# One encoder layer on one Trainium2 core: the first stage in blocks of 256 weight columns with fixed orders, and the forget gates' running sum on the Vector engine

## The chip, the cores and the metric

The kernel is one program on one core of a Trainium2 chip. A core has five engines that run side by side and meet only at semaphores: TensorE (PE; matmuls and transposes; its weight loads are listed as PEld), VectorE (DVE), ScalarE (ACT), GpSimd (POOL) and SyncE (SP, here used to issue DMAs). Data moves from HBM to the on-chip memory SBUF by DMA; TensorE writes only to PSUM, which has eight banks of 512 float32 columns on 128 partitions, and ACT and DVE read it from there. Each engine works through its own instruction stream in order: an instruction that waits holds up everything behind it on its engine.

The metric is the device time of one execution in microseconds (us). The time before is the median of three runs.

## The reference

The reference is one layer of a streaming encoder on 512 tokens of width 1024, in float32. Cut to what matters here:

```
h = rms_norm(x, norm_mix_pre)
a_q, a_k, a_v, f_q, f_k, f_v, f_g, c_u, s_x, s_b, s_c = split(h @ w_in)      # 5640 columns
ya = diff_attention(...);  ya = rms_norm(ya) * (1 - lambda_init)              # branch A, 4 heads
log_f = log_sigmoid(f_g + b_fgt);  c = cumsum(log_f, tokens)                  # branch F, 8 heads
yf = softmax(q k^T * scale + c[q] - c[k], causal) v
c_a, c_g = split(c_u + b_glu)                                                 # branch C
yc = silu(layer_norm(causal_depthwise_conv31(c_a * sigmoid(c_g))))
ys = s_b * causal_depthwise_conv3(s_c * s_x)                                  # branch S
mixed = sum_n sigmoid(h @ w_gate + b_gate)[n] * (branch[n] @ w_branch[n]) @ w_out
x = x + rms_norm(mixed);  cross-attention into 256 memory tokens;  gated MLP with a 3-tap conv
```

The change touches the first norm, the first products for `c_a` and `c_g`, and the running sum `c` of the eight forget gates over the tokens.

## The kernel before, in words

**Precision.** Every float32 operand of a product is split in two: `hi`, the value rounded to the matmul's fast format (a cast on ACT), and `lo`, what is left of it (a subtraction on DVE, sometimes on POOL). One product then is three passes on TensorE, hi x hi, hi x lo and lo x hi, accumulated in one PSUM bank (`mm3`, through `matmul`, L175). Weights come in pieces of 512 KB: `load_raw` (L120) issues the DMA on SP into one of two buffers `wr`; `split_weights` makes `wh` (L135, ACT) and `wl` (L136, on DVE or POOL), four buffers each.

**Layout.** Activations lie with channels on the partitions, as `ht` = (`hth`, `htl`), eight groups of 128 channels by 512 tokens. A token tile of x (128 tokens x 1024) is normed (`normed`: square sum on ACT L210, `rstd_of` on POOL L201 and L204, multiplication by the norm and by the gain on DVE L214), transposed by TensorE in groups of four 128x128 blocks (`to_channels`, `transpose` L179), and split from PSUM (`split`: ACT L109, DVE L110).

**Stages.** `all_jobs` lists the jobs of the layer; `run_blocks` loads and splits the weights of a job two jobs ahead and then runs its body. Work that isn't tied to weights (the convolution's 31 taps on DVE, attention heads, norms) is cut into pieces in a `Background` queue, which gives out pieces by a clock that counts the columns of the matmuls issued.

**What sets the order.** A planner arranges each engine's instructions by a simulated timeline, unless the kernel keeps some of them in the order of the program. In the kernel before, only ACT's instructions for the first two token tiles and the first weight cast are kept that way (`pin`), together with the DMAs of the small parameter rows (L298).

**First stage.** SP loads the gain row (L245), x tiles 0 and 1 (L247), the first 128 columns of the weights for `c_a`, and x tiles 2 and 3. TensorE spreads the gain row over the partitions (L256). Tiles 0 and 1 are normed and transposed. Then the first three blocks of `c_jobs` (128 columns of `c_a`, 128 of `c_g`, the next 128 of `c_a`) are multiplied with the first 256 tokens alone; tiles 2 and 3 are normed and transposed between them. After the third block the parameter rows are loaded (`load_rows`, L298) and transposed (`finish_init`), and the three blocks get the second 256 tokens. From the fourth block on a block takes all 512 tokens at once. `done` (L363, L366, L367) evacuates a block, and each finished pair of blocks starts a convolution task (L411, L415).

**Forget gates.** `forget_gates` computes the log-sigmoid on [128 tokens x 4 tiles x 8 heads] and then the sum over the tokens: four float32 products with a triangle of ones `tri` (L691) give [8 heads x 512 tokens] in PSUM. ACT scales it (L692), POOL writes it to DRAM as `crows` (L693), from where each pair of heads gets it spread over the partitions (`ck`, L710); four small transposes (L696) and a copy (L697) make `cq`. `f_task` builds the bias from both (POOL, L740 and L742) and adds it to the scores (DVE, L746).

## Time and profile before

| | us |
|---|---|
| median of three runs | 1111.14 |
| the three runs | 1110.30, 1112.38, 1111.14 |
| the profiled execution, its time | 1112.67 |
| the profiled execution, its span | 1111.0 |
| TensorE busy in that span | 1093.0 |
| DVE, ACT, POOL busy in that span | 690.5, 465.4, 107.4 |

The span is the time from the first to the last instruction that the profiler shows; the execution's own time has 1.67 us around it. In the profile, a group is named by line, engine and operation, then `out<-in` by the program's names and shapes. Matmuls are pipelined, so that the distance between two starts, and not the length of one, is the rate. The chain of waits is followed back from the last instruction, at each step to what released it. Idle time of an engine that is not the bottleneck costs nothing.

### The profile page before, as it was taken

The page shows a single profiled execution, that of the slowest core. Times are in us where ns is not written, and L with a number is a line of the kernel's source. Part 1 is how long each engine was busy: PE and PEld are TensorE (multiplying, and loading weights), DVE is VectorE, ACT ScalarE, POOL GpSimd, SP SyncE. Part 2 cuts the span into 40 slices and gives each one's busy share as a digit, 9 for nine tenths or more (in the row PEclk, how much of TensorE's full clock was granted, in tenths as well). Part 3 has the DMA queues.
Part 4 walks back from the last instruction along what each step waited for, and adds up shares of the span by engine and source line. Part 5 has one row for each costly group of instructions (what it writes and reads, how often), then busy time and mean ns, then how long its engine had stood idle before and what let it go on. Part 6 is the DMA issues. An engine that isn't in the chain of part 4 may idle for free.

```text
span 1111.0 us, 14146 instructions
## 1 busy us (share of the span) xinstructions
PE 1093.0 (98%) x5419; PEld 913.2 (82%) x5419; DVE 690.5 (62%) x1123; ACT 465.4 (42%) x783; POOL 107.4 (10%) x199
## 2 busy tenths in 40 slices
PE   7999999999999999999999999999999999999997
PEld 6888888887878978888888889888888888888886
DVE  4899985457665357767464477677666666642224
ACT  5322222467564255545442355454444444431112
POOL 3000001000101025323010130120000000000001
PEclk9999999999999999999999999999999999999999
DMA  6433433331212233333262252233333333332322
GB/s 176 119 93 97 104 89 94 95 95 58 76 58 77 77 115 95 96 95 92 79 201 89 90 171 97 94 95 113 96 95 95 95 95 95 95 95 95 95 76 76
DMA packets 147896, 109.29 MB, mean 98 GB/s; under 512 B 3647, under 2 KB 135340, under 8 KB 147829
## 3 DMA queue, kind: packets, MB, share of 16 engines
q1 hardware_dynamic: 145269, 99.85, 30.6%
q0 software_dynamic: 2560, 8.54, 2.7%
q8 instruction: 43, 0.70, 0.3%
q14 instruction: 24, 0.20, 0.1%
HBM read 106.27 MB, written 2.11 MB: 98 GB/s over the span
## 4 chain that ended last, share of the span: by engine, by line
PE 94%; DVE 2%; DMA 1%; POOL 1%; issue 1%; ACT 1%; POOLq 0%; DVEq 0%; SPq 0%; ACTq 0%
PE ps_mm L175 81%; PE ps_sc L175 7%; PE ps_tr L179 3%; PE ps_tr L175 3%; DVE wl L136 1%; POOL st_r L204 1%; DVE res L912 1%; DMA wr<-in_w_xkv 0%; DMA wr<-in_w_xq 0%; DMA xs<-in_x 0%; ACT nt L210 0%; POOL wl L136 0%; PE ps_sc L691 0%; ACT wh L135 0%; DVE e L579 0%
## 5 line engine op out<-in xcount | busy, mean ns | idle before, releaser
L175 PE MATMUL ps_mm<-hth,wh 128*128 128x512 f32 (+1 forms) x984 | 373.5, 380 | 1.6 <-ACT wh L135 1.2
L175 PE MATMUL ps_mm<-hth,wl 128*128 128x512 f32 (+1 forms) x984 | 373.0, 379 | 0.8 <-POOL wl L136 0.8
L175 PE MATMUL ps_mm<-htl,wh 128*128 128x512 f32 (+1 forms) x984 | 372.8, 379 | 0.3 <-DVE htl L110 0.3
L136 DVE TENSOR_TENSOR wl<-wr,wh 128x1024 fp32r<-128x1024 f32 (+1 forms) x180 | 221.4, 1231 | 231.4 <-ACT wh L135 228.5
L135 ACT CAST wh<-wr 128x1024 fp32r<-128x1024 f32 (+1 forms) x182 | 190.9, 1049 | 369.8 <-PE ps_mm L175 215.5
L175 PEld LDWEIGHTS ps_mm<-hth,wl 128*128 128x128 f32 x984 | 185.9, 189 | 36.3 <-POOL wl L136 1.0
L175 PEld LDWEIGHTS ps_mm<-hth,wh 128*128 128x128 f32 x984 | 185.9, 189 | 36.2 <-ACT wh L135 1.4
L175 PEld LDWEIGHTS ps_mm<-htl,wh 128*128 128x128 f32 x984 | 186.3, 189 | 34.8 <-DVE htl L110 0.5
L415 DVE SCALAR_TENSOR_TENSOR y<-y,par,y 128x482 f32<-128x482 f32 (+25 forms) x120 | 82.5, 729 | 0.2
L175 PE MATMUL ps_mm<-y,wh 128*128 128x512 f32 x256 | 80.9, 395 | 0.0
L352 DVE SCALAR_TENSOR_TENSOR c<-ps_mm,par,c 128x510 f32<-128x510 f32 x84 | 62.6, 746 | 1.4
L175 PEld LDWEIGHTS ps_mm<-y,wh 128*128 128x128 f32 x256 | 47.5, 188 | 9.9
L175 PE MATMUL ps_mm<-y,wl 128*128 128x512 f32 x128 | 50.8, 397 | 0.0
L201 POOL TENSOR_SCALAR st_m<-pm 128x1 f32<-128x1 f32 x12 | 2.6, 219 | 459.6 <-ACT junk L1164 349.2
L109 ACT CAST acth<-c 128x512 fp32r<-128x512 f32 x22 | 13.7, 620 | 54.8 <-DVE c L1111 54.8
L740 POOL TENSOR_SCALAR fbias<-ck,cq 128x128 f32<-128x128 f32 (+3 forms) x32 | 28.9, 907 | 69.9 <-DVE st L746 62.3
L175 PE MATMUL ps_mm<-wh,actl 128*128 128x512 f32 x88 | 34.6, 393 | 0.0
L175 PE MATMUL ps_mm<-wl,acth 128*128 128x512 f32 x88 | 34.6, 393 | 0.0
L175 PE MATMUL ps_mm<-wh,acth 128*128 128x512 f32 x88 | 34.2, 392 | 0.0
L109 ACT CAST pth<-ps_tr 128x512 fp32r<-128x512 f32 (+3 forms) x56 | 23.5, 450 | 23.9 <-PE ps_tr L179 22.6
L1105 ACT ACTIVATE c<-ps_mm,par 128x512 f32<-128x512 f32 x42 | 32.5, 773 | 0.0
L175 PE MATMUL ps_sc<-qk 128*128 128x128 f32 (+3 forms) x128 | 29.9, 329 | 1.1 <-DVE st L579 0.9
(268 smaller groups left out, 1573.5 us busy)
## 6 DMA issues: line engine op xcount, KB each, us to landing
wr<-in_w_up SPq DMA_DIRECT2D x44, 512.0 KB
wr<-in_w_in SPq DMA_DIRECT2D x40, 512.0 KB
wr<-in_w_gate SPq DMA_DIRECT2D x32, 512.0 KB
wr<-in_w_down SPq DMA_DIRECT2D x22, 512.0 KB
wr<-in_w_branch SPq DMA_DIRECT2D x16, 512.0 KB
wr<-in_w_out SPq DMA_DIRECT2D x8, 512.0 KB
wr<-in_w_xkv SPq DMA_DIRECT2D x8, 512.0 KB
wr<-in_w_in SPq DMA_DIRECT2D x4, 520.0 KB
```

The lines of the kernel that those rows point to most:

```text
L109: order(A.copy(hi, ps))
L135: order(A.copy(hi[:, :n], raw[:, :n]))
L136: low.tensor_tensor(lo[:, :n], raw[:, :n], hi[:, :n].bitcast(F32), ALU.subtract)
L175: PE.matmul(ps, lhs, rhs, start=start, stop=stop)
L179: PE.transpose(ps, x, ident[:n, :n])
L201: G.tensor_scalar(m, parts[0], EPS, None, ALU.add)
L204: G.tensor_tensor(r, m, nhalf[:, :n], ALU.pow)
L352: V.scalar_tensor_tensor(dst[:, s:], src[:, :S - s], w(k), dst[:, s:], ALU.mult, ALU.add)
L415: V.scalar_tensor_tensor(dst[:, s:], src[:, :S - s], pc("conv_dw", k * 4 + j), dst[:, s:], ALU.mult, ALU.add)
L740: G.tensor_scalar(bias[:, :w], ck[j][:, :w], -1.0, cq[:, qt, head:head + 1], ALU.mult, ALU.add)
L912: V.scalar_tensor_tensor(ns.out[t], scaled, rstd_of(ns.work, ms), src, ALU.mult, ALU.add)
L1105: A.activation(c[:, i], ps, AF.Identity, bias=pc("fb", ch), scale=pc("fdw2", ch))
```

## The change

- **Loads.** The first weights come as four transfers of 512 KB, each 4 channel groups (512 rows) by 256 columns: two for `c_a` (into two buffers of the tag `e`), two for `c_g` (into `wr`). SP issues, in kept order, the gain row, x tiles 0 and 1, the two `c_a` pieces, the two `c_g` pieces, x tiles 2 and 3, and the eleven parameter rows.
- **Norm of tiles 0 and 1.** The square sum is made in two halves, one on ACT and one on DVE; `rstd_of` adds both and the epsilon in one POOL instruction instead of two (this holds for the later norms with two parts as well).
- **Dummy matmuls.** `busy(n)` multiplies the identity with n columns of a mask in float32, into a bank that the first real product overwrites: one of 256 columns after the gain row, one of 128 after each of the first two groups of transposes.
- **Kept orders.** ACT, DVE, POOL and TensorE instructions of the first stage are kept in program order: the cast of the first `c_a` piece before the casts of the tokens, and so on as listed in the diff.
- **Passes one by one.** `first_half` runs one pass (hi x hi, then lo weights, then lo tokens) over 2 x 4 blocks of 128 columns and channel groups, on the first 256 tokens, and then the next pass. Tiles 2 and 3 are normed after the casts of `c_g` and transposed between its passes. The second 256 tokens of all four 128-column blocks are multiplied in `body_second`, by `mm3` as before.
- **Forget gates.** Four transposes bring the gates' values to [8 heads x 512 tokens] in PSUM, ACT scales them into SBUF, and one `tensor_tensor_scan` on DVE sums them along the tokens. The triangle and its products go.

The diff, cut to its core:

```diff
-        G.tensor_scalar(m, parts[0], EPS, None, ALU.add)
         if len(parts) == 2:
-            G.tensor_tensor(m, m, parts[1], ALU.add)
+            G.tensor_scalar(m, parts[0], parts[1], EPS, ALU.add, ALU.add)
+        else:
+            G.tensor_scalar(m, parts[0], EPS, None, ALU.add)
...
-    SP.dma_start(gain_row, a["norm_mix_pre"])
-    for t in range(NT):
-        SP.dma_start(xs[:, t], x_d[t * P:(t + 1) * P, :])
-        if t == 1:
-            w_first = load_raw(*glu_cols(0))
+    keep(SP.dma_start(gain_row, a["norm_mix_pre"]))
+    for t in range(2):
+        keep(SP.dma_start(xs[:, t], x_d[t * P:(t + 1) * P, :]))
+    raw_a = [e4() for _ in range(2)]
     for i in range(2):
-        PE.matmul(gain[i], ones, gain_row[:, i * 512:(i + 1) * 512], start=True, stop=True)
+        keep(SP.dma_start(blocks4(raw_a[i]), first_cols(O_CA, 4 * i)[0]))
+    raw_g = [load_raw(*first_cols(O_CG, 4 * i), keep) for i in range(2)]
+    for t in range(2, NT):
+        keep(SP.dma_start(xs[:, t], x_d[t * P:(t + 1) * P, :]))
...
-    y01 = [h_norm(0, pin), h_norm(1, pin)]
-    to_channels(y01[0], ht, 0, "tr", pin)
-    w_first = split_weights(*w_first, G, pin)
-    to_channels(y01[1], ht, 1, "mm", pin)
...
+    def busy(n):
+        keep(PE.matmul(glu[0][:, :n], ident, mask_a[:, :n], start=True, stop=True))
...
+        keep(A.activation(y_t[:, :512], xs[:, t, :512], AF.Square, scale=1.0 / math.sqrt(D), accum_out=parts[0]))
+        keep(V.tensor_tensor_reduce(y_t[:, 512:], xs[:, t, 512:], xs[:, t, 512:], scale=1.0 / D, scalar=0.0,
+                                    op0=ALU.mult, op1=ALU.add, accum_out=parts[1]))
...
+    busy(256)
...
+    def high_a(i):
+        keep(A.copy(wa[i][:, 0:2], raw_a[i]))
+    def low_a(i):
+        keep(G.tensor_tensor(wa[i][:, 2:4], raw_a[i], wa[i][:, 0:2].bitcast(F32), ALU.subtract))
...
+    def first_half(i, p, w, banks):
+        for c in range(2):
+            for k in range(4):
+                keep(PE.matmul(banks[c][:, :S // 2], w[p == 1][:, k, c * P:(c + 1) * P],
+                               ht[p == 2][:, i * 4 + k, :S // 2],
+                               start=(i, p, k) == (0, 0, 0), stop=(i, p, k) == (1, 2, 3)))
+    high_a(0)
+    low_a(0)
+    for t in range(2):
+        gained(t, 0)
+        turn(t, 0)
+        high(t, 0)
+        busy(128)
+    gained(0, 1)
+    gained(1, 1)
+    turn(0, 1)
+    first_half(0, 0, w_a[0], glu)
+    low(0, 0)
+    low(1, 0)
+    high(0, 1)
+    high_a(1)
+    low_a(1)
+    turn(1, 1)
+    high(1, 1)
+    low(0, 1)
+    low(1, 1)
+    first_half(0, 1, w_a[0], glu)
+    first_half(0, 2, w_a[0], glu)
+    for p in range(3):
+        first_half(1, p, w_a[1], glu)
+    casts = []
+    w_g = [split_weights(*raw, V, lambda ins: casts.append(keep(ins))) for raw in raw_g]
+    glu.extend(bank() for _ in range(2))
+    for i in range(2):
+        for p in range(3):
+            first_half(i, p, w_g[i], glu[2:])
+            if p == 2 - 2 * i:
+                with tc.issue_after(casts[-1].ins):
+                    y_t = normed(m1p, xs[:, 2 + i], gain, m1p.tile([P, D], F32, tag="ptl", name="nt", bufs=2))
+                to_channels(y_t, ht, 2 + i)
...
+        def body_second(hi, lo):
+            finish_init()
+            for j in range(2):
+                for part in range(2):
+                    ps = glu[part * 2 + j]
...
+                            mm3(ps[:, sl], w[0][:, k, c], w[1][:, k, c], ht[0][:, kk, sl], ht[1][:, kk, sl],
+                                kk == 0, kk == NK - 1)
+                    done(j, part, ps)
...
-        tri = m1p.tile([P, S], F32, tag="fbias", name="tri", bufs=2)
...
-            PE.matmul(pc_[:8, kt * P:], z[:, kt], tri[:, :n], start=kt == 0, stop=kt == NT - 1)
-        A.mul(row[:8, 0], pc_[:8, :], HD ** 0.5)
+            transpose(pz[:8, kt * P:(kt + 1) * P], z[:, kt])
+        A.mul(rz[:8, 0], pz[:8, :], HD ** 0.5)
+        V.tensor_tensor_scan(row[:8, 0], rz[:8, 1], rz[:8, 0], 0.0, ALU.mult, ALU.add)
```

In the diff, `gained`, `turn`, `high` and `low` of (tile, half) are the gain multiplication (DVE), four transposes (TensorE), the cast (ACT) and the remainder (DVE) of half a token tile.

## The prediction

> **What bounds the kernel now.** I read the page first: busy times, then the chain that ended last.

> ```profile
> PE 1093.0 (98%) x5419; PEld 913.2 (82%) x5419; DVE 690.5 (62%) x1123; ACT 465.4 (42%) x783; POOL 107.4 (10%) x199
> PE 94%; DVE 2%; DMA 1%; POOL 1%; issue 1%; ACT 1%; POOLq 0%; DVEq 0%; SPq 0%; ACTq 0%
> ```

> TensorE is busy for 1093.0 of 1111.0 us and carries 94% of the chain. So a change pays only where it takes instructions from TensorE, or lets its unbroken stream begin earlier. Next, who TensorE waited for in the first 40 us, apart from the load of the gain row at the very start (total us, times, longest):

> ```profile
> PE ps_tr L179 <- DVE nt L214: 1.6, 1, 1.6
> PE ps_mm L175 <- POOL wl L136: 0.8, 1, 0.8
> PE ps_mm L175 <- ACT hth L109: 0.4, 1, 0.4
> PE ps_mm L175 <- DVE htl L110: 0.3, 1, 0.3
> ```

> After 40 us its waits are short and scattered, and the change touches none of them. The chain of the first stage, in order of time (start, length, what):

> ```profile
> 1.19 3.65 DMA xs<-in_x
> 4.87 1.16 ACT nt L210 x2
> 6.11 0.24 POOL st_m L201
> 6.42 0.58 POOL st_r L204
> 7.02 0.76 DVE nt L214
> 7.83 1.98 PE ps_tr L179 x8
> 9.83 0.59 ACT hth L109
> 10.42 0.95 ACT wh L135
> 11.44 2.37 POOL wl L136
> 13.85 0.38 PE ps_mm L175
> ```

> The reader sees a ladder with one engine working at a time. Its last three rungs hurt: the first weights are rounded on ACT only after two token tiles' casts, their remainder takes 2.37 us on POOL, and the third matmul, which needs it, waits until 13.85. From there TensorE does not wait again in this stage. These rows tell its rate and where the first four convolution blocks end:

> ```profile
> 14.08 0.28 PE L175 MATMUL ps_mm<-hth,wh 128*128 128x256 f32 x1
> 14.78 0.41 PE L175 MATMUL ps_mm<-hth,wh 128*128 128x256 f32 x1
> 15.00 0.41 PE L175 MATMUL ps_mm<-htl,wh 128*128 128x256 f32 x1
> 17.77 0.41 PE L175 MATMUL ps_mm<-hth,wl 128*128 128x256 f32 x1
> 40.02 0.39 PE L175 MATMUL ps_mm<-hth,wh 128*128 128x512 f32 x1
> ```

> ```profile
> 15.00:20.00 5.00, 5.00 (x33) 5.00 (x32) 3.77 (x5) 2.58 (x4) 4.06 (x5) 0.68 0.48 125
> ```

> From 14.08 to 14.78 six matmuls of 256 columns start, one per 0.115 us. From 14.78 to 17.77 there are 15, one per 0.213 us: the granted clock is 0.68 over 15 to 20 us, half speed for some 3 us. That costs 15 x 0.098 = 1.5 us. The fourth block's eight weight groups are through at 40.02, so the stream from 13.85 lasts 26.2 us, or 24.7 at full clock.

> **The change part by part.** *Order of loads.* The first weights become four transfers of 512 KB ([4 groups of 128 rows] x 256 columns); the first stays third on SP's queue, behind two tiles of x. What the DMA moved in 0 to 14 us, in 40 slices of 0.35 us:

> ```profile
> GB/s 0 0 0 0 12 0 187 94 140 281 328 456 398 374 410 321 45 51 98 196 317 341 336 379 420 398 433 386 421 394 354 334 323 306 247 162 69 0 0 0
> ```

> Summed, two tiles of x are in by 5.6 us; the next 0.52 MB need the four slow slices and three and a bit of the following: about 7.85 us. At some 370 GB/s one more transfer lands every 1.4 us: second half of the first weights 9.3, gate halves 10.7 and 12.1, x tiles 2 and 3 at 13.5 and 14.9. SP also issues the eleven small parameter rows before any later weight instead of after three blocks. What queues behind them, the weights of the fifth block, is used only at about 36 us, and its two buffers are not free before the gate halves are split, near 15; I cost the move at nothing, and 1 us at most if that cover went.

> *The norm of tiles 0 and 1.* Each square sum is shared: half on ACT, half on DVE, then one POOL addition of both. The nearest rows for the halves, with those of the later steps:

> ```profile
> L579 DVE CUSTOM_DVE_ANT_0 e<-ps_sc,mask_a x32: 277/486/692, 240.5 to 333.5; 128x128 f32<-128x128 f32 x8, 128x256 f32<-128x256 f32 x8, 128x384 f32<-128x384 f32 x8, 128x512 f32<-128x512 f32 x8
> ```

> ```profile
> L135 ACT CAST wh<-wr 128x1024 fp32r<-128x1024 f32 x11 | 11.6, 1050 | 24.7 <-PE ps_mm L175 16.0 <-DMA wr<-in_w_in 4.9 <-DVE y L411 3.8
> L136 POOL TENSOR_TENSOR wl<-wr,wh 128x1024 fp32r<-128x1024 f32 x2 | 4.7, 2370 | 3.2 <-ACT wh L135 3.2
> L110 DVE TENSOR_TENSOR htl<-ps_tr,hth 128x512 fp32r<-128x512 f32 x6 | 4.0, 684 | 0.3
> L109 ACT CAST hth<-ps_tr 128x512 fp32r<-128x512 f32 x6 | 3.5, 586 | 3.0 <-PE ps_tr L179 2.8
> ```

> The DVE half (0.69 and its accumulator read, say 0.08) runs 4.87 to 5.65, POOL's two steps and their gaps 0.95, to 6.6, the first gain multiply 0.75, to 7.38. That is 0.4 us ahead of the 7.78 of before. POOL's new addition with two pointers has no row: at least the 0.19 of the addition it replaces, at most 0.19 + 0.24; I take 0.24, the one-pointer form.

> *ACT and POOL, in kept order.* The first cast of weights is put ahead of every cast of tokens: 7.9 + 1.05 = 8.95; then the two first-half token casts, 9.55 and (if transposed by then) 10.15. This is a new wait: token casts queue behind a transfer. POOL's remainder runs 8.95 to 11.3, 2.5 us earlier than now.

> *TensorE.* Gain rows end at 6.26, a dummy fp32 matmul follows, and one of half the length after each of the first two groups of four transposes:

> ```profile
> 2.51 3.75 PE L256 MATMUL ps_sc<-gain_row,ones 1*128 1x512 f32 x4 [2.51 <-DMA gain_row<-in_norm_mix_pre]
> 18.92 0.44 PE ps_tr L179 x4
> ```

> The chain's 1.98 for eight transposes at 7.83, against 0.44 for four at 18.92, says that the array is still at half speed there. Cold, four are 0.85; by the four 512-column passes (0.94 each) a 256-column dummy, two such passes of half the length, is 0.9 and a 128-column one 0.45. The walk: dummy 6.3 to 7.2; transposes 7.4 to 8.3; dummy 8.7; transposes 9.6; dummy 10.0; transposes 10.85. So the first real matmul starts at 10.85 if cold and at 10.15 (ACT) if fast throughout. I take 10.8: half speed ending near 10.6, because TensorE now has only 0.2 us of idleness after 2.5, where before it had 1.6 us ahead of 7.83.

> *The passes one by one.* High x high for all eight groups first (0.92 us, to 11.7), four more transposes, then the weight remainder (ready 11.3), then the token remainder (two at 0.68 after 9.55 and 10.15: ready by 11). The second half of the weights: cast by 11.8, POOL 14.2, wanted at 14.9. Gate halves: casts by 14.4, DVE remainders by 16, wanted at 16.8. Nothing is late, so the stream from 10.8 holds the work of the one of before, two matmuls (0.23) and four transposes (0.44) more: 24.7 + 0.67 = 25.4, to 36.2 instead of 40.02. **Gain 3.8 us.** Its ends: 4.4 (10.15), and 0.7 (half speed to 14.1 as before, and a second slow stretch, both below).

> *Forget gates.* Before, the sum along the tokens is four fp32 products with a triangle on TensorE:

> ```profile
> 397.84 0.40 PE L175 MATMUL ps_mm<-htl,wh 128*128 128x512 f32 x1
> 398.17 2.32 PE L691 MATMUL ps_sc<-tri,fz 128*8 128x512 f32 x8
> 400.42 0.51 PE L175 MATMUL ps_mm<-hth,wl 128*128 128x512 f32 x1
> ```

> ```profile
> 400.52 0.59 ACT L692 ACTIVATE e<-ps_sc 8x512 f32<-8x512 f32 x1 [1.21 <-PE ps_sc L691]
> 409.33 0.29 DVE L746 CUSTOM_DVE_ANT_0 e<-ps_sc,fbias 128x128 f32<-128x128 f32 x1 [3.02 <-POOL fbias L742]
> ```

> At 0.23 a product the next would have started at 398.07; it started at 400.42: 2.35 us. Four transposes of 8 columns take their place, at most the 0.44 of four full ones. **Gain 1.9 us.** The ACT copy stays; behind it DVE gets a scan of 512 steps without a row here: not under the 0.69 of a 512-wide DVE operation, and up to 2.37, the slowest 1024-element row; I take 1.2, two steps' time each. The chain to the bias then starts about 1.9 - 1.2 us sooner; its reader at 409.33 is a DVE operation, and TensorE shows no wait on it. [...]

> *The rest.* The one-step addition also serves the later norms. There the first addition was done early, so on the last chain 0.19 becomes 0.24:

> ```profile
> 1105.58 0.19 POOL L203 TENSOR_TENSOR st_m<-st_m,pm 128x1 f32<-128x1 f32 x1 [2.62 <-ACT junk L1164]
> ```

> Loss 0.05. **Sum: -3.8 - 1.9 + 0.05 = -5.65 us.** The profiled execution spans 1111.0 and took 1112.67, 1.5 above the median of 1111.14; against itself it would be 1107.0, against the median 1105.5.

> **The rivals.** *Half speed lasts.* Transposes may count little as activity; then half speed lasts from 10.85 to about 14.1, where it ended before. 3.25 us at half speed do 1.6 us of work: the stage gains 2.2, the sum is -4.0, **1107.1**. With another slow stretch like the one at 14.78 it is -2.6, **1108.5**. For it: 3.75 us of gain matmuls left the transposes slow. Against it: in 7.83 to 13.85 nearly all of TensorE's work was transposes, and 14.08 is at full speed. [...]

> *The stage's gain is hidden*: something off TensorE sets the pace after 40 us. The candidate is DVE:

> ```profile
> 31.00:100.00 69.00, 69.00 (x317) 56.96 (x316) 66.89 (x97) 20.04 (x24) 0.00 (x0) 1.00 0.40 102
> ```

> It is busy for 66.89 of 69 us with convolution taps. But TensorE is busy for all 69 and no wait on a DVE weight remainder stands in its list. Then only the gates pay: -1.85, **1109.3**.

> *Slower*: with DVE this full, a new order that puts a weight remainder behind a burst of taps stalls TensorE in each of some 12 blocks of 5.5 us in that stretch. It decides for slower by over 0.2% once the blocks lose 5.65 + 2.2 = 7.9 us, 0.65 each; at 0.75 each the time is 1111.14 - 5.65 + 9 = **1114.5**. Against it: tap work per block is given out by TensorE's own count, which the change leaves as it was.

> **How the numbers follow.** My forecast has 0.59, lasting half speed 0.26, the hidden gain 0.08, slower 0.07. About 0.2%, 2.2 us, is what a measurement of this kernel can tell from no change (its three runs lie between 1110.3 and 1112.38). The first two cases end under 1108.9: faster 0.85; hidden is the same, with the edge of the second: 0.09; slower 0.06. The range goes from 1103.7 (10.15 as the start, -6.3, and a run spread of 1.1 below) to 1109.1 (the second case's worse end and 0.6).

> **What would show it.** The profile after should have the first 256-column matmul near 10.8, rows 0.115 apart soon after it, no wait of TensorE over 0.5 us between 11 and 36, and the second-half products of the first four blocks done near 36.2. At the gates four transposes of some 0.1 us should stand where L691 stood, and a DVE scan of about 1.2. I would be wrong if the first cast of weights starts much after 7.9, if TensorE waits for POOL's remainder or for kept casts, if spacing stays at 0.213 after 11, or if new waits on DVE stand between 40 and 240 us.

## The result, and the profile after

| | before | after |
|---|---|---|
| median, us | 1112.26 (20 runs on the chip of the comparison) | 1109.03 (20 runs) |
| profiled execution: time, span | 1112.67, 1111.0 | 1108.61, 1106.8 |
| TensorE busy | 1093.0 | 1091.0 |

The changed kernel takes 0.9973 of the time before (95% interval 0.9967 to 0.998): 3.2 us less by the medians. The forecast was 5.65 us less, 1105.5; the result lies at the upper edge of the range, 1103.7 to 1109.1.

The page of the changed kernel: busy times, then the chain that ended last.

```profile
PE 1091.0 (99%) x5445; PEld 913.1 (82%) x5445; DVE 693.9 (63%) x1128; ACT 464.9 (42%) x783; POOL 97.9 (9%) x186
PE 94%; DVE 2%; DMA 1%; issue 1%; ACT 1%; POOL 0%; POOLq 0%; DVEq 0%; SPq 0%; ACTq 0%
```

TensorE still carries the chain, so the time is read from TensorE's stream alone. The chain of the first stage (start, length, what), changed kernel:

```profile
5.66 0.31 POOL st_m L205
6.04 1.12 POOL st_r L208
7.18 0.76 DVE nt L338
7.99 1.12 PE ps_tr L343 x4
9.10 0.43 PE ps_mm L310 x2
9.53 0.85 PE ps_tr L343 x4
10.38 0.43 PE ps_mm L310 x2
10.81 0.85 PE ps_mm L343 x4
11.66 1.71 PE ps_mm L359 x8
13.37 0.84 PE ps_mm L343 x4
14.21 7.63 PE ps_mm L359 x64
```

The ladder of waits across engines is gone: from 7.99 on it is TensorE alone, and no step waits for ACT's cast, for POOL's remainder or for a transfer. But it starts late, through POOL's power (1.12 us, where the row of before had 0.58), it holds two dummies of 0.43, and the first eight real products take 1.71 us (half speed), against 7.63 / 8 = 0.95 for eight of the 64 from 14.21 on.

TensorE's own rows, first product and the place where the four blocks end (start, length, engine, line, operation):

```profile
11.31 2.06 PE L359 MATMUL ps_mm<-hth,wa 128*128 128x256 f32 x8
13.17 1.04 PE L343 MATMUL ps_mm<-ident,nt 128*128 128x128 f32 x4
13.87 1.29 PE L359 MATMUL ps_mm<-hth,wa 128*128 128x256 f32 x8
38.31 0.40 PE L178 MATMUL ps_mm<-hth,wh 128*128 128x512 f32 x1
```

The first four blocks are through at 38.31, before at 40.02: 1.7 us gained in this pair of executions. At the gates (same columns):

```profile
396.39 0.40 PE L178 MATMUL ps_mm<-htl,wh 128*128 128x512 f32 x1
396.63 0.60 PE L182 MATMUL ps_sc<-ident,fz 128*8 128x128 f32 x4
396.98 0.48 PE L178 MATMUL ps_mm<-hth,wl 128*128 128x512 f32 x1
399.05 1.21 DVE L782 TENSOR_TENSOR_SCAN e<-e 8x512 f32<-8x512 f32 x1
```

The next product was due 0.23 us after 396.39 and starts at 396.98: 0.36 us lost, before 2.35. The scan takes 1.21 us, and no wait of TensorE hangs on it.

What is new stands at 267 us. TensorE's waits from 240 to 290 us in total (what, for whom, us, times, longest), first before, then after:

```profile
PE ps_tr L179 <- DVE e L589: 1.0, 1, 1.0
PE ps_sc L175 <- DVE st L579: 0.3, 1, 0.3
```

```profile
PE ps_tr L182 <- DVE e L681: 1.8, 2, 1.0
PE ps_sc L178 <- DVE st L671: 0.6, 2, 0.3
PE ps_mm L178 <- DVE ptl L110: 0.2, 1, 0.2
```

The second wait for `e` and the one for `ptl`, 1.0 us together, belong to the second softmax head. These rows (timeline) show what they hang on, first before, then after:

```profile
268.74 0.48 DVE L589 SCALAR_TENSOR_TENSOR e<-e,st 128x256 f32<-128x256 f32 x1
269.31 0.39 PE L175 MATMUL ps_mm<-hth,wl 128*128 128x512 f32 x1
270.59 1.23 DVE L136 TENSOR_TENSOR wl<-wr,wh 128x1024 fp32r<-128x1024 f32 x1 [0.22 <-ACT wh L135]
```

```profile
267.02 1.22 DVE L139 TENSOR_TENSOR wl<-wr,wh 128x1024 fp32r<-128x1024 f32 x1
268.16 0.48 DVE L681 SCALAR_TENSOR_TENSOR e<-e,st 128x256 f32<-128x256 f32 x1
268.62 0.69 DVE L110 TENSOR_TENSOR ptl<-ps_tr,pth 128x512 fp32r<-128x512 f32 x1
268.78 0.41 PE L182 MATMUL ps_tr<-ident,e 128*128 128x128 f32 x2 [0.77 <-DVE e L681]
```

A weight remainder of 1.22 us now stands on DVE ahead of the operation that TensorE's next transposes wait for. In the kernel before, the same remainder (the 47th of the program in both) came behind it. TensorE's own order differs too. Before, five weight products (268.31 to 269.54, the last of them in the row above) stand between the head's four transposes at 267.96 and the next two at 270.00, and cover what DVE does. After, the last such product starts at 265.27, ahead of the four transposes at 266.21, and none is left to cover the wait. No line of the softmax was edited: the planner re-arranged the steps.

### The profile page after: what moved, and what is told of

It is laid out like the page before. It is cut to its first block, busy times and chain, and to the rows that moved or that the text cites. A ratio compares the mean times of both kernels' runs of the same rounds, so it can differ in the third digit from the quotient of the medians.

```text
span 1106.8 us, 14168 instructions
## 1 busy us (share of the span) xinstructions
PE 1091.0 (99%) x5445; PEld 913.1 (82%) x5445; DVE 693.9 (63%) x1128; ACT 464.9 (42%) x783; POOL 97.9 (9%) x186
## 4 chain that ended last, share of the span: by engine, by line
PE 94%; DVE 2%; DMA 1%; issue 1%; ACT 1%; POOL 0%; POOLq 0%; DVEq 0%; SPq 0%; ACTq 0%
PE ps_mm L178 80%; PE ps_sc L178 7%; PE ps_tr L182 3%; PE ps_tr L178 3%; PE ps_mm L359 1%; DVE wl L139 1%; DMA wr<-in_w_xo 1%; DMA wr<-in_w_xkv 0%; ACT wh L138 0%; DMA xs<-in_x 0%; POOL st_r L208 0%; DVE e L671 0%; PE ps_tr L343 0%; PE ps_mm L343 0%; ACT hth L109 0%
## 5 line engine op out<-in xcount | busy, mean ns | idle before, releaser
L178 PE MATMUL ps_mm<-htl,wh 128*128 128x512 f32 (+1 forms) x944 | 359.9, 381 | 0.0
L178 PE MATMUL ps_mm<-hth,wh 128*128 128x512 f32 (+1 forms) x944 | 359.8, 381 | 0.0
L178 PE MATMUL ps_mm<-hth,wl 128*128 128x512 f32 (+1 forms) x944 | 358.7, 380 | 0.0
L138 ACT CAST wh<-wr 128x1024 fp32r<-128x1024 f32 (+1 forms) x180 | 188.6, 1050 | 349.1 <-PE ps_mm L178 223.0
L178 PEld LDWEIGHTS ps_mm<-hth,wl 128*128 128x128 f32 x944 | 177.4, 188 | 34.5
L178 PEld LDWEIGHTS ps_mm<-hth,wh 128*128 128x128 f32 x944 | 177.6, 188 | 33.9
L178 PEld LDWEIGHTS ps_mm<-htl,wh 128*128 128x128 f32 x944 | 177.6, 188 | 33.0
L507 DVE SCALAR_TENSOR_TENSOR y<-y,par,y 128x499 f32<-128x499 f32 (+28 forms) x120 | 82.7, 729 | 0.2
L205 POOL TENSOR_SCALAR st_m<-pm,pm 128x1 f32<-128x1 f32 x12 | 4.6, 387 | 480.6 <-ACT junk L1254 357.0
L109 ACT CAST acth<-c 128x512 fp32r<-128x512 f32 x22 | 13.7, 621 | 55.2 <-DVE c L1201 55.2
L109 ACT CAST pth<-ps_tr 128x512 fp32r<-128x512 f32 (+3 forms) x56 | 23.7, 451 | 27.8 <-PE ps_tr L182 24.9
L110 DVE TENSOR_TENSOR ptl<-ps_tr,pth 128x512 fp32r<-128x512 f32 (+3 forms) x56 | 27.8, 512 | 9.5 <-ACT pth L109 9.1
L830 POOL TENSOR_SCALAR fbias<-ck,cq 128x128 f32<-128x128 f32 (+3 forms) x32 | 25.5, 805 | 70.6 <-DVE st L836 66.9
```

Source lines behind the costliest of these rows:

```text
L109: A.copy(hi, ps)
L110: V.tensor_tensor(lo, ps, hi.bitcast(F32), ALU.subtract)
L138: order(A.copy(hi[:, :n], raw[:, :n]))
L178: PE.matmul(ps, lhs, rhs, start=start, stop=stop)
L205: G.tensor_scalar(m, parts[0], parts[1], EPS, ALU.add, ALU.add)
L507: V.scalar_tensor_tensor(dst[:, s:], src[:, :S - s], pc("conv_dw", k * 4 + j), dst[:, s:], ALU.mult, ALU.add)
```

## The experiments

Each was timed against the kernel before on the same chip, and profiled in one execution. "Start of the scores" below is TensorE's first score product, up to which all these kernels have the same real work (the new stage does the fourth block in two halves of the tokens, 24 products more but no more columns); from there to the gates' product or transposes all have the same 851.

### One half of the change at a time

The gates alone: the kernel before, with the lines of the sum replaced.

```diff
-            PE.matmul(pc_[:8, kt * P:], z[:, kt], tri[:, :n], start=kt == 0, stop=kt == NT - 1)
-        A.mul(row[:8, 0], pc_[:8, :], HD ** 0.5)
+            transpose(pz[:8, kt * P:(kt + 1) * P], z[:, kt])
+        A.mul(rz[:8, 0], pz[:8, :], HD ** 0.5)
+        V.tensor_tensor_scan(row[:8, 0], rz[:8, 1], rz[:8, 0], 0.0, ALU.mult, ALU.add)
```

> The kernel before with the gate edit alone: four transposes and a scan instead of the triangle products. If the gates' gain is TensorE time on the path, the distance between the two 512-column products around them falls from 2.35 us (398.07 to 400.42) to about 0.35, and the time falls by 2.0 us (ratio 0.998). The rival, that the later scan delays the bias and the scores wait for it, gives no change (ratio 1.000) and a TensorE wait on the bias or on DVE near 410 us.

> The kernel before with the edit at the gates alone, timed and profiled a second time. Theory A (2.0 us less of TensorE's time is 2.0 us less of the whole): the time is 1.6 to 2.4 us below that of before, and the first measurement of 0.85 was low by chance. Theory B (part of it is given back after the gates): again about 0.85 below, and the profile shows TensorE waiting about 1.1 us more than before does in the cross attention between 640 and 745 us.

Measured 1111.26 and, the second time, 1111.89: ratios 0.9991 (0.9982 to 1.0) and 0.9993 (0.9985 to 1.0002), 0.7 to 0.9 us gained. Yet TensorE's gap at the gates falls here too by 2.0 us (four transposes at 396.31, the next product at 396.67). The rest is given back at 648 us, where TensorE waits for the weights of the cross-attention. Waits from 640 to 665 us, in the kernel before and in the second profile of the gates alone:

```profile
PE ps_mm L175 <- ACT wh L135: 1.9, 2, 1.2
```

```profile
PE ps_mm L175 <- ACT wh L135: 3.1, 3, 1.2
```

In a second execution of the kernel before they are 0.8 us, in the first profile of the gates alone 2.3: on average 2.7 against 1.35. ACT's cast there waits for a transfer (the second profile of the gates alone):

```profile
649.00 1.04 ACT L135 CAST wh<-wr 128x1024 fp32r<-128x1024 f32 x1 [5.46 <-DMA wr<-in_w_xkv]
```

SP issues this transfer sooner, as much as TensorE is ahead, but from its issue to the cast it is 5.1 and 6.1 us here (641.29 to 646.36, 642.94 to 649.00), and 4.4 and 4.0 in the kernel before (645.06 to 649.41, 645.02 to 649.02). So a slower landing takes back about 1.3 of 2.0 us; what slows it was not tried. In the changed kernel it lands 4.2 us after its issue, and the wait is 0.7 (0.6 in its second profile).

The stage alone: the changed kernel with the triangle's products.

```diff
-            transpose(pz[:8, kt * P:(kt + 1) * P], z[:, kt])
+            PE.matmul(pc_[:8, kt * P:], z[:, kt], tri[:, :n], start=kt == 0, stop=kt == NT - 1)
```

> The changed kernel with the triangle products put back, so the rebuilt first stage alone. By the profile of the changed kernel the first four blocks end at 38.3 instead of 40.0 us: the time falls by 1.7 us (ratio 0.9985). If the stage's gain is given back later (DVE sets the pace after 40 us), the first blocks end at 38.3 all the same and the time is that of before (ratio 1.000). If my forecast of the stage was right and its profile an unlucky one, 3.8 us (0.9966).

Measured 1111.03, ratio 0.999 (0.9982 to 0.9999). The triangle's building had slipped between POOL's two weight remainders, and TensorE waited 0.41 us for the second of them. So it was run again with that building kept behind both:

```diff
-        G.memset(tri, 1.0)
+        keep(G.memset(tri, 1.0))
```

> The new first stage alone, with the triangle of ones built on POOL behind both weight remainders, which it slipped between before. The computation is that of the reference. Theory A (that slip cost 0.4 to 1.2 us of the stage): no wait of TensorE on POOL's remainder over 0.2 us in the first 40 us, and a time 1.4 to 2.2 below before. Theory B (the stage is worth 1.0 whatever POOL does): 1.0 below before again.

Measured 1110.97, ratio 0.9987 (0.9979 to 0.9996): 1.6 us below its own before, the wait on POOL gone. The changed kernel, timed in the same series, took 1109.19, so that the gates are worth 1.8 us by the medians on top of the new stage. The new waits at 268 us (1.8 us in all for `e` from 240 to 290 us, instead of 1.0) are in both kernels with the stage alone and in neither profile of the gates alone: they come with the stage.

### The same two programs once more

The kernels before and after, unedited, in a second execution each.

> The kernel before, profiled in a second execution. Theory A (my prediction missed because the stage of before is not one number): TensorE's slow stretch after 14.8 us is chance, and without it TensorE reaches the second block of weights near 17.3 and waits for their cast about 0.9 us, as in the profile with the gate edit alone. Then the first four blocks end between 39 and 40.1 here too. Theory B (before's 40.02 held 1.5 us of bad luck and the stage has nothing to give): they end near 38.6. Time 1112.1 in both.

> The changed kernel, profiled in a second execution. Theory A (TensorE's full speed comes at a moment that differs between executions): the first product starts at 11.7 again, the spacing falls from 0.213 to 0.115 us anywhere between 11 and 14.2, and the first four blocks end between 37.0 and 38.3 accordingly. Theory B (it is fixed by the work done before, so 14.2 belongs to this program): spacing 0.213 up to 14.2 again and the end at 38.3. Time about 1109.1 in both.

Measured 1112.27 and 1109.19, ratio 0.9972 (0.9961 to 0.9983). Before: TensorE's slow stretch after 14.5 us is there again; only the first profile of the gates alone lacks it. (In the second one half speed simply lasted: products 0.213 us apart up to 18.9 us, and the trace's first record of full speed at 19.86. The granted clock reads 1.00 ahead of a trace's first record, so that early on the spacing decides.) From 14 to 18 us (busy us and instructions of PE, PEld, DVE, ACT, POOL; granted clock; DMA share; GB/s), the second execution of before, then the gates alone:

```profile
14.00:18.00 4.00, 4.00 (x21) 4.00 (x22) 2.72 (x4) 1.55 (x4) 3.73 (x5) 0.57 0.51 131
```

```profile
14.00:18.00 4.00, 3.81 (x32) 3.58 (x32) 2.72 (x4) 1.65 (x4) 3.75 (x5) 1.00 0.51 131
```

Where the stretch is missing, TensorE arrives early at the second block and waits 0.95 us for its cast, at 18.76: the old stage gains only 0.5 us by it (start of the scores 237.87 against 238.39). So the 1.5 us of the slow stretch were rightly counted as the old stage's: no profile of the new stage shows such a stretch between its first record of full speed and 250 us. After: full speed came earlier this time, with the first product (second execution of the changed kernel):

```profile
11.49 1.20 PE L359 MATMUL ps_mm<-hth,wa 128*128 128x256 f32 x8
12.53 0.60 PE L343 MATMUL ps_mm<-ident,nt 128*128 128x128 f32 x4
37.34 0.40 PE L178 MATMUL ps_mm<-hth,wh 128*128 128x512 f32 x1
```

Eight products in 1.04 us instead of 1.86, and the four blocks end at 37.34 instead of 38.31. One program, two executions, 1 us apart.

### Dummies

Without the three dummies:

```diff
-    busy(256)
-        busy(128)
```

> The changed kernel without the three dummy matmuls. Theory one, the clock: the float32 dummies and the transposes do not bring the array to full speed, so without them full speed comes at the same 14 us, the first product starts 0.5 us earlier (at about 11.2, then ACT's casts end), and the time is 0.2 to 0.3 us below the changed kernel's. [...]

Measured 1109.29, ratio 0.9975 (0.9966 to 0.9984), as with them. The first product starts at 10.93 instead of 11.31, at half speed. But that start isn't the dummies' doing alone. The transposes begin at 7.62 instead of 7.99, because POOL's power for tile 0 took 0.57 us here and 1.11 in the changed kernel. The rows of the changed kernel, then of this one:

```profile
6.03 0.69 DVE L317 CUSTOM_DVE_ANT_0 nt<-xs 128x512 f32<-128x512 f32 x1 [0.57 <-DMA xs<-in_x]
6.04 1.11 POOL L208 TENSOR_TENSOR st_r<-st_m,nhalf 128x1 f32<-128x1 f32 x1
```

```profile
6.08 0.57 POOL L208 TENSOR_TENSOR st_r<-st_m,nhalf 128x1 f32<-128x1 f32 x1
6.21 0.69 DVE L317 CUSTOM_DVE_ANT_0 nt<-xs 128x512 f32<-128x512 f32 x1 [0.70 <-DMA xs<-in_x]
```

Where tile 1's square sum on DVE begins up to 0.02 us ahead of the power or with it, the power takes 1.10 to 1.13 us (six profiles); where the power begins 0.01 to 0.13 us ahead, 0.57 (four). The square sum begins when tile 1 lands, so that each execution decides it anew. In time, the dummies of the change buy nothing and cost little.

In the one-pass format (one instruction in the trace for each dummy; a float32 one has two, `L310 x2` in the chain above):

```diff
-        keep(PE.matmul(glu[0][:, :n], ident, mask_a[:, :n], start=True, stop=True))
+        keep(PE.matmul(glu[0][:, :n], dz[:, :P], dz[:, :n], start=True, stop=True))
-    busy(256)
+    for _ in range(4):
+        busy(512)
```

> The changed kernel with its dummies in the one-pass format of the real products (ones times ones, 512 columns each: four behind the gain row, one after each of the first two groups of transposes), about the same wall time as before. Theory one, that what counts for the clock is dense one-pass products and not float32 dummies or transposes: full speed by 10.6 or sooner, first product at about 11.2 and 0.115 us apart at once, first four blocks done near 36.6, time 1.7 us below the changed kernel's (ratio to before 0.996). Rival, that full speed comes at a fixed moment near 14 us whatever runs before: spacing stays at 0.213 until 14 and the time is that of the changed kernel (0.9973).

Measured 1113.31, ratio 1.0008 (0.9999 to 1.0017). This run was badly made: filling `dz` on DVE pushed the filling of `ones` behind the square sums, and the gain rows came at 6.96 instead of 2.24 us. It says nothing on the time. Mended, with `dz` filled on POOL, three dummies of 512 columns behind the gain rows and one of 256 and one of 512 behind the first two groups of transposes:

> The changed kernel with its three dummies in the one-pass format and denser: three of 512 columns behind the gain rows, one of 256 and one of 512 behind the first two groups of transposes. The order at 267 us is the changed kernel's. Theory A (dense products bring full speed before the first real product): the first eight products take 1.05 us or little more in the profile, not 1.7, and the time is 0.4 to 1.0 below the changed kernel's, 1108.2 to 1108.8. Theory B (the 5.6 us that the last kernel won came from the order at 267 us alone): 1109.0 to 1109.5.

Measured 1108.36, ratio 0.9965 (0.9952 to 0.9978), against 0.9973 (0.9967 to 0.998) for the changed kernel: some 0.8 us less, as theory A has it, but the intervals overlap, so that the time doesn't decide. The rows of this kernel:

```profile
6.05 1.65 PE L313 MATMUL ps_mm<-wa 128*128 128x512 f32 x3
10.73 1.22 PE L362 MATMUL ps_mm<-hth,wa 128*128 128x256 f32 x8
11.79 0.60 PE L346 MATMUL ps_mm<-ident,nt 128*128 128x128 f32 x4
```

The first eight products take 1.06 us. Over all profiles: with dense one-pass dummies these eight took 1.04 to 1.33 us in five kernels of five; without, 1.04 to 1.38 in five and 1.85 to 1.87 in four of nine. That fits a clock that dense products release; with 0 in 5 against 4 in 9 it is not proof. The traces' records of the clock add that full speed came 4.1 to 5.6 us after the first dense dummy in all five, in the badly made kernel too, where that dummy came 4.6 us later (at 10.67, full speed at 14.92; 10.2 to 11.6 in the other four): it is not a fixed moment near 14 us. Not all of the early start here is the clock's: the power took 0.57 us in this profile, and the transposes began at 7.51 instead of 7.99.

### The start of the walk

Tile 1's square sum wholly on ACT, no dummies, and the first cast of tokens ahead of the first cast of weights:

```diff
+        if t == 0: keep(V.tensor_tensor_reduce(y_t[:, 512:], xs[:, t, 512:], xs[:, t, 512:], ...
-    high_a(0)
-    low_a(0)
     for t in range(2):
         gained(t, 0)
         turn(t, 0)
         high(t, 0)
+        if t == 0: high_a(0); low_a(0)
```

> The changed kernel without dummies, with tile 1's square sum wholly on ACT, so that POOL's power for tile 0 doesn't run beside a square sum on DVE, and with the first cast of tokens ahead of the first cast of weights on ACT. The computation is that of the reference. Theory A (the first product is late by TensorE's dummies and by the 1.11 us power on POOL): the power takes 0.57 us, the first product of 256 columns starts at 10.2 to 10.7 instead of 11.3 to 11.5, and the time is 0.5 to 1.0 below the changed kernel's, about 1108.4. Theory B (the landing of the first weights at 9.1 and their cast bind next): the first product not before 10.9 and a time within 0.3 of the 1109.25 of the kernel without dummies.

Measured 1109.08, ratio 0.9972 (0.996 to 0.9983). POOL's power takes 0.57 us as expected, and tile 0's gain multiplication comes at 6.89 instead of 7.18, although tile 0 landed 0.25 us later here. But tile 1's square sum ends later on ACT alone, its gain multiplication starts at 8.42, TensorE waits 0.42 us for it, and the first product came at 11.02. Theory B in its time; what bound, though, was tile 1's norm.

### The order at 267 us

The remainder on POOL:

```diff
+        count.append(1); low = G if len(count) in (45,) else low
         low.tensor_tensor(lo[:, :n], raw[:, :n], hi[:, :n].bitcast(F32), ALU.subtract)
```

> The changed kernel with one weight remainder (the one that stands on DVE at 267 us, ahead of the second step of the second softmax head's pair) on POOL, which is idle there. The computation is that of the reference. Theory A (the new stage's gain is partly given back at that place, because the planner now puts this remainder of 1.22 us ahead of the operation that TensorE's transposes wait for): TensorE's two waits there, 0.8 and 0.2 us, vanish, and the time is 0.9 to 1.7 below that of the changed kernel, 1107.4 to 1108.2. Theory B (the wait is only moved: the POOL remainder takes 2.4 us and is late, or the next step of the head waits instead): within 0.3 of 1109.1.

Measured 1112.00, ratio 0.9995 (0.9986 to 1.0004): by the ratios some 2.4 us worse than the changed kernel, which neither theory had. The rows of this kernel:

```profile
267.21 2.37 POOL L139 TENSOR_TENSOR wl<-wr,wh 128x1024 fp32r<-128x1024 f32 x1 [14.15 <-DVE st L671]
267.57 2.29 DVE L681 SCALAR_TENSOR_TENSOR e<-e,st 128x256 f32<-128x256 f32 x1
```

The DVE operation, 0.48 us in the changed kernel, takes 2.29 beside POOL's subtraction and ends 0.28 us behind it; TensorE waits 1.45 us for it instead of 0.77. More follows: the granted clock is 0.60 from 272 to 276 us, and 0.71 from 268 to 272 in the next kernel, which has the same wait; no other kernel here shows a fall of the clock between 260 and 280 us. The place is on the path, the cure was wrong. Together with the walk:

> Both edits above in one kernel. The computation is that of the reference. If each removes what it names: 1106.5 to 1107.5. If only the softmax head's wait is worth something: 1107.4 to 1108.2. If neither: 1109.

Measured 1111.11, ratio 0.9993 (0.9983 to 1.0002): the walk's gain none, POOL's loss again (the same operation took 2.28 us).

The order restored on DVE, by issuing the remainder behind that operation:

```diff
+            with tc.issue_after(e_ops[-1].ins):
+                f()        # the 45th remainder
```

> The changed kernel with one order restored: the weight remainder on DVE at 267 us is issued behind the softmax operation that it stood ahead of, as in the kernel before, and stays on DVE. Nothing else is edited. Theory A (the new stage's gain is given back there): TensorE's wait of 0.8 us for that operation goes, and the time is 0.7 to 1.7 below the changed kernel's, 1107.4 to 1108.5. Theory B (the softmax head is bound by something else, and the remainder is missed where it was): within 0.3 of 1109.15.

Measured 1110.46, ratio 0.9984 (0.9975 to 0.9993): no gain, and theory A falls in this form. TensorE's waits from 262 to 276 us are 0.8 and 0.2 us in the changed kernel, as above, and in this one:

```profile
PE ps_mm L185 <- ACT pth L109: 0.7, 1, 0.7
```

The wait for DVE went and one for ACT came, whose cast of `pth` is next in line. So DVE's order alone doesn't make the loss. TensorE's order is still the changed kernel's here: its last weight product starts at 266.60, ahead of the head's four transposes at 267.54, and nothing covers the steps behind them. With dense dummies beside it:

> The changed kernel with the dense dummies and with the order at 267 us restored. Theory A (two separate causes that add): the gains of the two kernels above added, 1106.5 to 1107.6. Theory B (one hides the other): no better than the better of the two.

Measured 1109.14, ratio 0.9971 (0.9959 to 0.9983), no better than the dummies alone.

Then the kernel in which the planner, fed another first stage, puts cast and remainder behind that head's steps by itself: the walk and dense dummies, first with the one remainder on POOL (where it now runs later, beside nothing that matters), then without.

> The same with dummies in the one-pass format on TensorE: three of 512 columns behind the gain rows, one of 256 between the two groups of four transposes and one of 512 behind them. The computation is that of the reference. Theory A (full speed comes a few us after dense products begin, whatever stands between): every profile shows the first products of 256 columns 0.115 us apart, and the time is 0.3 to 0.8 below that without dummies. Theory B (the moment is set by something else than TensorE's work, and dummies only take time): 0.3 to 0.6 above that without dummies.

> The fastest kernel so far without its remainder on POOL. The planner by itself puts the remainder behind the softmax operation here, as in the kernel before. Theory A (first stage and order make the time): 1105.2 to 1106.2, as with the remainder on POOL. Theory B (POOL's help made it): 1107 to 1109.

Measured 1105.54 (ratio 0.9943, 0.993 to 0.9955) and 1105.63 (0.9942, 0.9928 to 0.9956): the fastest kernels here, 6.5 and 6.2 us below their own before, where the changed kernel is 3.2 and 3.4 below its. Neither theory of the first had that: it is 5.6 below the same kernel without dummies, not 0.3 to 0.8, and the clock can't be all of it. POOL has no visible part in it. TensorE's waits from 240 to 290 us in the latter:

```profile
PE ps_tr L182 <- DVE e L685: 1.0, 1, 1.0
PE ps_sc L178 <- DVE st L675: 0.6, 2, 0.3
```

The new wait is not there, and TensorE has seven weight products (263.64 to 265.13) between the head's transposes, where the kernel before has five. How much that is worth shows in the time from the start of the scores to the gates, 851 instructions in each, in profiles with a granted clock of 1.00 from 252 to 260 us: gates alone, changed kernel, and this one.

```profile
237.87 0.22 PE L175 MATMUL ps_sc<-qk 128*128 128x128 f32 x1
396.31 0.60 PE L179 MATMUL ps_sc<-ident,fz 128*8 128x128 f32 x4
```

```profile
236.75 0.22 PE L178 MATMUL ps_sc<-qk 128*128 128x128 f32 x1
```

```profile
235.41 0.22 PE L178 MATMUL ps_sc<-qk 128*128 128x128 f32 x1
393.11 0.60 PE L182 MATMUL ps_sc<-ident,fz 128*8 128x128 f32 x4
```

That is 158.4 us with the old order, 159.9 (to 396.63) in the changed kernel, 160.0 with dense dummies (234.95 to 394.99), and 157.7 in the fastest. The changed kernel gives back 1.4 us in this stretch, 1.0 of it in the two waits at 268 us.

## Why the prediction was right or wrong

| step | forecast | measured |
|---|---|---|
| first weights landed | 7.85 | 9.1, not waited for |
| first product | 10.8 | 11.31, 11.49 |
| half speed ends | 10.6 | 14.1 and 11.5 |
| four blocks done | 36.2 | 38.31, 37.34 |
| gap at the gates | 0.44 | 0.36 |
| scan | 1.2 | 1.21 |
| waits after 40 us | unchanged | 1.0 us new at 268 |

**Right.** The sign, the mechanism of both parts, and the gates' term: 1.9 forecast, 2.0 in TensorE's rows, 1.8 in time on top of the new stage (0.7 to 0.9 alone). The triangle's products had been on the path and the scan is not. The scan's 1.2 us, for which the forecast had no row, was the author's choice between 0.69 and 2.37; its row after shows 1.21. No step of the first stage waits for ACT's kept casts, for POOL's remainder or for a transfer, though the weights landed 1.3 us later than worked out and their cast began at 9.11 instead of 7.9, which the prediction had named as a sign of being wrong; the late start of the walk hid it. From 5.6 to 9.1 us the DMA moved 253 GB/s, 0.89 MB, of which this transfer is 0.52: other transfers took a share, where the sum had let them come one after another. The slow stretch after 14.8 us was the old stage's own in three profiles of four.

**The term that was mis-sized** is the stage's 3.8 us. Over four profiles with the old stage the scores start at 238.52 on average, over five with the new one, its dummies and no other stall in it at 236.21: 2.3 us gained (2.0 without the old profile in which half speed lasted to 19.86). Three parts fell short in the profile shown. The start: 11.31 instead of 10.8, mainly since POOL's power took 1.11 us behind tile 1's square sum on DVE and not the 0.57 that it takes when it begins first, and the addition with two pointers 0.30 instead of 0.24. The clock: half speed until 14.1 costs 0.8 us in the first eight products and 0.35 in the next transposes; this is the rival "half speed lasts", which that profile followed and the next one did not, so that it is a matter of the execution and not of the program. That the time lies near the 1108.5 of this rival's worse end is chance, since the second slow stretch of that sum never came. And 0.4 us in the stream itself, 25.8 instead of 25.4. The 10.6 of the forecast was the author's estimate, argued from 0.2 us of idleness ahead of the walk: TensorE idled 0.84 us there (its transposes at 7.99 waited for DVE's `nt`), half speed ended at 14.1 and 11.5 in two executions, and that idle time decides it was not shown.

**The step that failed** is "After 40 us its waits are short and scattered, and the change touches none of them". The planner arranges all later work anew when the first stage is another, and it put a weight block's cast and remainder among the steps of the second softmax head, and no longer TensorE's products of a block between them: 1.4 us given back at equal clock, with the same waits of 0.8 and 0.2 us in both its profiles. The rival "slower" had this mechanism, a remainder placed badly on DVE, but looked for it in the convolution's blocks at twelve places; it came once, at 268 us, behind the 40 to 240 us in which the prediction had looked for new waits on DVE. With 2.3 + 1.9 - 1.4 the sum is 2.8; the medians say 3.2. What is left, 0.4, is not explained. It is not the work behind the gates: from the first product there to the end of the span it is 710.6 and 709.5 us in the two profiles of before, 709.9 and 710.2 in those of the changed kernel. A fall of the clock near 250 us, which both profiles of before and one of the two after have, shifts the stretch by more than that (last section).

**Open.** Why the planner prefers the one order or the other at 267 us was not tried, nor could a single order be restored with a gain: restoring DVE's brought ACT's wait forward. TensorE's own order, which in the kernel before and in the fastest one puts weight products between the head's steps, was not restored by itself; that it is the cause is argued from the rows and not shown. That the order as a whole is worth 1.4 to 2.3 us is shown by the interval above, in kernels that also differ in the first stage.

## What to carry to other kernels

Where a planner lays out the whole program, an edit in one stage moves work in all of them: forecast the edit's own term, then add a term of either sign for the new layout, and after the run compare TensorE's waits stage by stage between marks with equal work. A gain can be taken back at a later place where TensorE waits for a transfer: here about 1.3 of 2.0 us, at 648 us. Two instructions on two engines that begin within 0.13 us of each other can make a stage that differs from profile to profile: POOL's power took 1.10 to 1.13 us or 0.57, by whether DVE's square sum or the power began first. Before work is moved to an idle engine, see what runs on the others at that moment: a DVE operation of 0.48 us took 2.29 beside the subtraction that was moved to POOL.

## What was unexpected of the hardware

```profile
252.00:256.00 4.00, 3.23 (x11) 2.27 (x12) 3.75 (x19) 3.05 (x11) 1.04 (x2) 0.71 0.39 131
```

```profile
252.00:256.00 4.00, 3.70 (x18) 2.83 (x17) 3.17 (x13) 4.00 (x14) 1.04 (x2) 1.00 0.35 122
```

  The granted clock is 0.71 and 1.00. The stretch from the start of the scores to the gates is 159.8 us with it and 158.4 without, old order; in the changed kernel 159.9 without it and 161.1 with it, in two executions of one program. Some 1.2 us between executions have nothing to do with an edit. In the traces' records of the clock every such fall lasts 3.41 us (253.69 to 257.11 in the first profile of before), and the time from the rise ahead of it to the fall is a whole multiple of that: 235.52 us (69 times) in both profiles of before, 238.93 (70 times) in most of the others.
- In nine profiles of the new stage without dense dummies, the moment of full speed in these records lay between 11.07 and 14.06 us: 3.0 us apart, less than one such 3.41, and 2.6 apart in two executions of one program.
